# One place in the scheduler's order for all matmuls of a projection's PSUM tile, in a two-block transformer kernel

## The chip, the cores and the metric

The kernel runs on one core of one Trainium2 chip, in one launch. The metric is the device time of one execution in microseconds (us), taken as the median over several executions. The core has TensorE (PE) for matmuls, VectorE (DVE), ScalarE (ACT) and GpSimd (POOL) for elementwise work, SyncE (SP), which mostly issues DMAs, and 16 DMA engines. In the profile PEld is the loading of TensorE's stationary operand, which overlaps the matmuls.

## The reference

512 tokens of width 1024 go through two blocks, all in fp32. The first block has two layers; each has four attention kinds side by side and a feed-forward part of width 4096:

```python
for l in range(DEPTH):                       # 2 layers
    h = rms_norm(x, norm1[l])
    proj = h @ w_in[l]                       # 1024 x 2764, split into 16 parts
    ...                                      # o_a latent, o_b window, o_c top-k, o_d forget-gate attention
    x = x + mixed @ w_out[l]
    h2 = rms_norm(x, norm2[l])
    x = x + jnp.square(jax.nn.relu(h2 @ w_up[l])) @ w_down[l]
```

The second block normalizes x (with a scale and shift made from a condition vector by the ada weights), projects it to the parts of a gated delta rule (8 heads, chunks of 64), of a dilated window attention (12 heads) and to gates, and ends with three output projections whose results are combined and normalized.

## The kernel before, in words

**A projection.** Activations are kept transposed, channels on the 128 partitions and the 512 tokens in the free dimension. One output tile of a projection is 128 channels by 512 tokens in one PSUM bank, the tile `g`; `gtile` (line 139) gives it out of three buffers. To keep fp32 precision, every operand is split into a high and a low part of the reduced type fp32r. `split` (lines 122 to 136) does this for the weights: ACT copies the raw chunk to `whi` (line 130), and the remainder `wlo` is made by DVE (line 133) or POOL (line 135); each has three buffers (`split_bufs`), in the down projections of the feed-forward part four (`db`, tags `dh` and `dl`). The activations are split into `hh` and `hl` (line 160/161) or, in the feed-forward part, `sh` and `sl`. `gemm` (lines 141 to 152) then issues, for each 128-deep slice k of the inner dimension, three matmuls of 128x128 by 128x512: high by high (line 149), high weights by low activations (line 150), low weights by high activations (line 151). With 8 slices a tile has 24 matmuls, in `e_out` and the down projections with 4 slices it has 12. Weights come from HBM in pieces of 1 MB or less into `raw`, which has two buffers.

**The order of the work.** The program text only lists the operations. A list scheduler, which simulates the engines while the program is built, puts each engine's instructions into a fixed order; among instructions that it deems ready it takes the one with the smallest priority number. The number is a counter, `cur_priority`, that goes up by one with each instruction issued in the text. `gemm` raises it by `gp` (700 in the first block, 600 in the second) so that projections fill gaps left by the chains of the attention, and sets it back to its old value at the end (line 152). So the matmuls of one tile get rising numbers, `old + gp`, `old + gp + 1` and on, and the next projection, issued a handful of instructions later in the text, starts its numbers only a few places above the first one's start. On the chip each engine then takes its instructions in the fixed order.

**The stages.** The page's time runs through: attention of layer one (0 to 340 us), its feed-forward part (340 to 700), attention of layer two (700 to 1010), its feed-forward part, in which DVE also works off the ada products (1010 to 1385), the second block (1385 to 2000) and the final stage (from 2000). An attention stage begins with projections of the indexer's queries, of small pieces and of the latents (`qi`, `misc`, `Aq`, `Ak` in the list at line 815). `e_out` (line 802) adds the output projection to x and sums squares (`sumsq_add`, lines 166 to 172: ACT squares, POOL adds). The feed-forward part loops over 8 chunks of 512 hidden channels: `up(ch + 1)`, four tiles whose results DVE takes out of PSUM (line 860), and then `down(ch)`, eight tiles that DVE adds into `xT` (line 882). The last chunk has no `up` ahead of its `down`. After each layer, a matmul with ones (`ssp`, line 179, or line 996 at the end of the second layer) sums the squares over the channels. In two places the projections are not by `gemm`: `values` (line 549) and the delta block's V for the first group (line 1444), where `old` is read once and four tiles are issued in a loop.

Of the kernel before, what the change touches and what calls it, by code (L numbers as in the profile page):

```python
# [43 lines left out]
class Kernel:  # L44
# [96 lines left out]
    def gemm(self, ps, wk, acts, nk, first=True, last=True):  # L141

        nc = self.nc
        old = self.tc.cur_priority
        self.tc.cur_priority = old + self.gp
        for k in range(nk):
            wh, wl = wk(k)
            ah, al = acts(k)
            nc.tensor.matmul(ps, wh, ah, start=first and k == 0, stop=False)  # L149
            nc.tensor.matmul(ps, wh, al, start=False, stop=False)  # L150
            nc.tensor.matmul(ps, wl, ah, start=False, stop=last and k == nk - 1)  # L151
        self.tc.cur_priority = old


    def fold(self, x, g, d):
# [234 lines left out]
    def attn(self, l, hs, ssq, xin, xout):  # L390
# [30 lines left out]
        def raw_in(off, n=256):  # L421
            return self.raw(w_in[:, off:off + n], KD, n)
# [126 lines left out]
        def values(off):  # L549
            raw = raw_in(off)  # L550
            his = []
            for kk in range(2):
                his.append(self.split([(full, raw[:, 4 * kk:4 * kk + 4, :])], [P, 4, 256], lo=los.pop(0)))
            V = ap.tile([P, NB, 256], F32, name=self.nm("V"), tag="V", bufs=2)
            old = self.tc.cur_priority
            for b in range(NB):
                ps = self.gtile()
                self.tc.cur_priority = old + self.gp
                for k in range(KD):
                    wh, wl = (t[:, k % 4, :] for t in his[k // 4])  # L560
                    ah, al = (t[:, HB(b)] for t in hs[k])
                    nc.tensor.matmul(ps[:, :256], ah, wh, start=k == 0, stop=False)  # L562
                    nc.tensor.matmul(ps[:, :256], ah, wl, start=False, stop=False)
                    nc.tensor.matmul(ps[:, :256], al, wh, start=False, stop=k == KD - 1)
                self.tc.cur_priority = old
                nc.scalar.activation(V[:, b, :], ps[:, :256], AF.Copy, scale=S["rnat"][:, b:b + 1])
            return V
# [127 lines left out]
        def e_DV():  # L695
            S["VD"] = values(O_DV)
# [78 lines left out]
        def e_CV():  # L775
            S["VC"] = values(O_CV_)
# [655 lines left out]
    def g_Dv(self, gi, hs):  # L1432
        nc = self.nc
        w = self.I["w_in_2"][0]
        c0 = 4112 + 1536 + 256 * gi
        raw = self.raw(w[:, c0:c0 + 256], KD, 256)
        V = self.dst[gi]["V"] = self.da.tile([P, NB, 256], F32, name=self.nm("V"), tag="V", bufs=1)
        if gi:
            for j in range(2):
                t = self.residues(self.proj2(raw, slice(j * P, (j + 1) * P), hs), gi)  # L1440
                nc.scalar.activation(V[:, :, j * P:(j + 1) * P], self.natural(t), AF.Copy)
                yield
            return
        his = [self.split([(lambda t: t, raw[:, 4 * kk:4 * kk + 4, :])], [P, 4, 256], lo="v") for kk in range(2)]
        old = self.tc.cur_priority
        for b in range(NB):
            sel = lambda t: t[:, b * P:(b + 1) * P]
            ps = self.gtile()
            self.tc.cur_priority = old + self.gp
            for k in range(KD):  # L1450
                wh, wl = (t[:, k % 4, :] for t in his[k // 4])
                ah, al = (sel(t) for t in hs[k])
                nc.tensor.matmul(ps[:, :256], ah, wh, start=k == 0, stop=False)
                nc.tensor.matmul(ps[:, :256], ah, wl, start=False, stop=False)
                nc.tensor.matmul(ps[:, :256], al, wh, start=False, stop=k == KD - 1)
            self.tc.cur_priority = old
            nc.scalar.activation(V[:, b, :], ps[:, :256], AF.Copy)
            if b % 2:
                yield
# [341 lines left out]
```

## Time and profile before

| | |
|---|---|
| median of 3 runs | 2178.02 us (2175.59 to 2180.3) |
| the profiled execution | 2177.57 us, its span 2175.8 us |
| mean granted TensorE clock, share of full speed | 0.979 |
| PE busy | 2035.3 us, 94% of the span |
| DVE, ACT, POOL busy | 60%, 45%, 16% |
| DMA | 243.97 MB, mean 112 GB/s |
| chain that ended last | PE 65%, DVE 17%, DMA 6%, ACT 6%, issue 4%, POOL 2% |

The span is the time from the first to the last instruction of the profiled execution. TensorE's matmuls are pipelined, and a matmul's shown duration overlaps the next one's; what a matmul costs is read as the distance between two starts. A number in brackets behind a timeline entry is the time that the engine stood still ahead of it, with the instruction that released it.

### The profile page before, as it was taken

How to read it: one execution, taken by the hardware profiler on the slowest of the kernel's cores; microseconds unless marked ns; L12 is line 12 of the kernel's file. 1: busy time of each engine (PE TensorE's matmuls, PEld its weight loads, DVE VectorE, ACT ScalarE, POOL GpSimd, SP SyncE). 2: the span in 40 equal slices, each digit the busy share in tenths (PEclk: the TensorE clock that was granted, in tenths of full speed). 3: DMA queues.
4: the chain of work that ended last, by engine and by line, in shares of the span. 5: the costliest groups of instructions: out<-in, count | busy, mean ns of one | idle time of the engine just before them, and what ended most of it. 6: DMA issues, size and time to landing. Idle time of an engine off the chain costs nothing.

```text
span 2175.8 us, 27326 instructions
## 1 busy us (share of the span) xinstructions
PE 2035.3 (94%) x10015; PEld 1574.6 (72%) x10015; DVE 1315.3 (60%) x2372; ACT 973.6 (45%) x1769; POOL 350.5 (16%) x282
## 2 busy tenths in 40 slices
PE   6988989999999898999999999799999999999798
PEld 5776767777777676776777777577667767777576
DVE  6488764444444578855665554785484684763554
ACT  4546654222323454754332223563565655645332
POOL 5226320000003324511000000310102011000000
PEclk8999999999999999999999999999999999999899
DMA  5332443223323342352543433232213222244762
GB/s 173 99 102 73 132 145 116 78 79 98 115 78 93 98 110 78 93 167 81 172 149 125 136 116 108 69 98 80 75 64 97 76 71 89 87 139 159 263 207 97
DMA packets 230647, 243.97 MB, mean 112 GB/s; under 512 B 43771, under 2 KB 186026, under 8 KB 230514
## 3 DMA queue, kind: packets, MB, share of 16 engines
q1 hardware_dynamic: 227826, 240.13, 35.6%
q10 hardware_dynamic: 2688, 2.10, 0.3%
q8 instruction: 79, 1.29, 0.2%
q14 instruction: 54, 0.44, 0.1%
HBM read 203.93 MB, written 31.04 MB: 108 GB/s over the span
## 4 chain that ended last, share of the span: by engine, by line
PE 65%; DVE 17%; DMA 6%; ACT 6%; issue 4%; POOL 2%; SPq 0%; DVEq 0%; ACTq 0%; POOLq 0%
PE g L149 16%; PE g L150 15%; PE g L151 15%; DVE wlo L133 3%; PE oT L322 2%; DMA raw<-in_w_up_dram 1%; DVE X L1271 1%; PE pt L313 1%; DMA raw<-in_ada_w_dram 1%; DVE pr L1269 1%; ACT whi L130 1%; PE g L562 1%; PE S L678 1%; DVE m L543 1%; PE S L386 1%
## 5 line engine op out<-in xcount | busy, mean ns | idle before, releaser
L130 ACT ACTIVATE whi<-raw 128x1024 fp32r<-128x1024 f32 (+3 forms) x302 | 297.8, 1001 | 661.6 <-PE g L150 450.8
L149 PE MATMUL g<-hh,whi 128*128 128x512 f32 (+1 forms) x1368 | 497.7, 405 | 16.0 <-ACT whi L130 3.1
L151 PE MATMUL g<-hh,wlo 128*128 128x512 f32 x1368 | 487.5, 400 | 7.9 <-DVE wlo L133 7.8
L150 PE MATMUL g<-hl,whi 128*128 128x512 f32 x1368 | 490.4, 399 | 0.0
L133 DVE TENSOR_TENSOR wlo<-raw,whi 128x1024 fp32r<-128x1024 f32 (+4 forms) x258 | 309.2, 1212 | 129.6 <-ACT whi L130 114.0
L149 PEld LDWEIGHTS g<-hh,whi 128*128 128x128 f32 (+1 forms) x1368 | 259.3, 190 | 93.2 <-issue 15.6
L151 PEld LDWEIGHTS g<-hh,wlo 128*128 128x128 f32 x1368 | 258.1, 189 | 69.0 <-DVE wlo L133 10.0
L150 PEld LDWEIGHTS g<-hl,whi 128*128 128x128 f32 x1368 | 259.4, 190 | 55.2 <-issue 3.7
L149 PE MATMUL g<-sh,whi 128*128 128x512 f32 x512 | 195.5, 404 | 8.4 <-DVE xT L882 6.6
L150 PE MATMUL g<-sl,whi 128*128 128x512 f32 x512 | 190.9, 392 | 0.0
L151 PE MATMUL g<-sh,wlo 128*128 128x512 f32 x512 | 187.7, 391 | 0.0
L135 POOL TENSOR_TENSOR wlo<-raw,whi 128x1024 fp32r<-128x1024 f32 x44 | 107.1, 2435 | 424.7 <-ACT whi L130 284.2
L882 DVE TENSOR_TENSOR xT<-xT,g 128x512 f32<-128x512 f32 x128 | 85.8, 686 | 133.7 <-PE g L151 133.5
L149 PEld LDWEIGHTS g<-sh,whi 128*128 128x128 f32 x512 | 95.9, 188 | 48.6 <-DVE xT L882 22.6
L172 POOL TENSOR_TENSOR ssq<-sq,ssq 128x512 f32<-128x512 f32 x35 | 52.2, 1493 | 446.4 <-ACT sq L171 445.7
L860 DVE SCALAR_TENSOR_TENSOR r<-g,rstd 128x512 f32<-128x512 f32 x64 | 43.9, 690 | 122.3 <-PE g L151 122.3
L151 PEld LDWEIGHTS g<-sh,wlo 128*128 128x128 f32 x512 | 96.1, 188 | 21.4 <-DVE wlo L133 0.3
L150 PEld LDWEIGHTS g<-sl,whi 128*128 128x128 f32 x512 | 96.2, 188 | 17.9
L310 ACT ACTIVATE L<-L,mn 128x256 f32<-128x256 f32 (+3 forms) x128 | 68.4, 536 | 41.6 <-DVE mn L309 40.9
L318 ACT ACTIVATE ptsb<-pt 128x256 f32<-128x256 f32 (+3 forms) x128 | 50.9, 412 | 41.7 <-PE pt L313 38.5
L322 PE MATMUL oT<-ptsb,V 128*64 128x128 f32 x592 | 65.8, 289 | 3.2 <-ACT mx L575 3.1
L861 ACT ACTIVATE r<-r 128x512 f32<-128x512 f32 x64 | 40.0, 629 | 47.1 <-DVE r L860 46.9
(447 smaller groups left out, 3289.1 us busy)
## 6 DMA issues: line engine op xcount, KB each, us to landing
raw<-in_w_in_dram SPq DMA_DIRECT2D x46, 1024.0 KB
raw<-in_w_up_dram SPq DMA_DIRECT2D x32, 1024.0 KB
raw<-in_w_down_dram SPq DMA_DIRECT2D x32, 1024.0 KB
raw<-in_ada_w_dram SPq DMA_DIRECT2D x12, 1024.0 KB
raw<-in_w_in_dram SPq DMA_DIRECT2D x22, 512.0 KB
raw<-in_w_out_dram SPq DMA_DIRECT2D x32, 256.0 KB
fd<-f SPq DMA_DIRECT2D x30, 256.0 KB
xd<-xT SPq DMA_DIRECT2D x24, 256.0 KB
```

Source lines behind the costliest of these rows:

```text
L130: nc.scalar.activation(f(hi), src, AF.Copy)
L133: nc.vector.tensor_tensor(f(lw), src, f(hi), ALU.subtract)
L135: nc.gpsimd.tensor_tensor(f(lw), src, f(hi), ALU.subtract)
L149: nc.tensor.matmul(ps, wh, ah, start=first and k == 0, stop=False)
L150: nc.tensor.matmul(ps, wh, al, start=False, stop=False)
L151: nc.tensor.matmul(ps, wl, ah, start=False, stop=last and k == nk - 1)
L172: nc.gpsimd.tensor_tensor(ssq, sq, ssq, ALU.add)
L310: nc.scalar.activation(L[:, :n], L[:, :n], AF.Exp, bias=m, scale=-1.0, accum_out=sm[:, hh, i:i + 1])
L318: nc.scalar.activation(pts_[:, :n], pt[:, :n], AF.Copy)
L322: nc.tensor.matmul(oT[hh * 64:(hh + 1) * 64, i * P:(i + 1) * P], V(hh, j0 + jj), pts[hh][:, jj * P:(jj + 1) * P], start=jj == 0, stop=jj = ...
L860: nc.vector.scalar_tensor_tensor(r, ps, 0.0, rstd, ALU.max, ALU.mult)
L882: nc.vector.tensor_tensor(x, x, ps, ALU.add)
```

## The change

A method `later(old)` sets the counter to `old + gp`, and it is called ahead of every matmul of a projection instead of once ahead of the tile's first one. All 24 (or 12) matmuls of a tile thus carry the same number; the next tile's number is higher, since its `old` is. No instruction, shape or buffer changes, only the order.

```diff
--- before.py
+++ after.py
@@ -142,14 +142,20 @@
 
         nc = self.nc
         old = self.tc.cur_priority
-        self.tc.cur_priority = old + self.gp
         for k in range(nk):
             wh, wl = wk(k)
             ah, al = acts(k)
+            self.later(old)
             nc.tensor.matmul(ps, wh, ah, start=first and k == 0, stop=False)
+            self.later(old)
             nc.tensor.matmul(ps, wh, al, start=False, stop=False)
+            self.later(old)
             nc.tensor.matmul(ps, wl, ah, start=False, stop=last and k == nk - 1)
         self.tc.cur_priority = old
+
+    def later(self, old):
+
+        self.tc.cur_priority = old + self.gp
 
 
     def fold(self, x, g, d):
@@ -555,12 +561,14 @@
             old = self.tc.cur_priority
             for b in range(NB):
                 ps = self.gtile()
-                self.tc.cur_priority = old + self.gp
                 for k in range(KD):
                     wh, wl = (t[:, k % 4, :] for t in his[k // 4])
                     ah, al = (t[:, HB(b)] for t in hs[k])
+                    self.later(old)
                     nc.tensor.matmul(ps[:, :256], ah, wh, start=k == 0, stop=False)
+                    self.later(old)
                     nc.tensor.matmul(ps[:, :256], ah, wl, start=False, stop=False)
+                    self.later(old)
                     nc.tensor.matmul(ps[:, :256], al, wh, start=False, stop=k == KD - 1)
                 self.tc.cur_priority = old
                 nc.scalar.activation(V[:, b, :], ps[:, :256], AF.Copy, scale=S["rnat"][:, b:b + 1])
@@ -1446,12 +1454,14 @@
         for b in range(NB):
             sel = lambda t: t[:, b * P:(b + 1) * P]
             ps = self.gtile()
-            self.tc.cur_priority = old + self.gp
             for k in range(KD):
                 wh, wl = (t[:, k % 4, :] for t in his[k // 4])
                 ah, al = (sel(t) for t in hs[k])
+                self.later(old)
                 nc.tensor.matmul(ps[:, :256], ah, wh, start=k == 0, stop=False)
+                self.later(old)
                 nc.tensor.matmul(ps[:, :256], ah, wl, start=False, stop=False)
+                self.later(old)
                 nc.tensor.matmul(ps[:, :256], al, wh, start=False, stop=k == KD - 1)
             self.tc.cur_priority = old
             nc.scalar.activation(V[:, b, :], ps[:, :256], AF.Copy)
```

The places below show TensorE's instructions in the order of before and of the changed kernel. A name's number tells apart the tiles; in the changed kernel lines 150 and 151 of before are lines 151 and 153. The numbers in g, sh, sl, whi and wlo are the same tiles in both.

The first place is the end of the second layer's last down projection: g_10878, g_10892 and g_10906 are the last three of its eight tiles, and ssp_10950 the sum over channels of the squares of the finished x. TensorE before:

```order
L150 MATMUL g_10906<-sl_10587,whi_10800 128x512
L150 MATMUL g_10878<-sl_10623,whi_10804 128x512
L149 MATMUL g_10892<-sh_10622,whi_10804 128x512
L151 MATMUL g_10906<-sh_10586,wlo_10801 128x512
L151 MATMUL g_10878<-sh_10622,wlo_10805 128x512
L150 MATMUL g_10892<-sl_10623,whi_10804 128x512
L149 MATMUL g_10906<-sh_10622,whi_10804 128x512
L151 MATMUL g_10892<-sh_10622,wlo_10805 128x512
L150 MATMUL g_10906<-sl_10623,whi_10804 128x512
L151 MATMUL g_10906<-sh_10622,wlo_10805 128x512
L996 MATMUL ssp_10950<-ssqb,ones 128x512
```

TensorE after the change:

```order
L149 MATMUL g_10906<-sh_10548,whi_10794 128x512
L151 MATMUL g_10906<-sl_10549,whi_10794 128x512
L153 MATMUL g_10906<-sh_10548,wlo_10795 128x512
L149 MATMUL g_10906<-sh_10586,whi_10800 128x512
L151 MATMUL g_10906<-sl_10587,whi_10800 128x512
L153 MATMUL g_10906<-sh_10586,wlo_10801 128x512
L149 MATMUL g_10906<-sh_10622,whi_10804 128x512
L151 MATMUL g_10906<-sl_10623,whi_10804 128x512
L153 MATMUL g_10906<-sh_10622,wlo_10805 128x512
L1004 MATMUL ssp_10950<-ssqb,ones 128x512
```

Before, the three tiles take turns and all end within the last six matmuls ahead of ssp; now the last tile's matmuls stand together, and g_10892 and g_10878 ended 12 and 24 matmuls ahead of its end.

The second place is the start of layer one's attention: g_274 and g_303 are the two halves of the indexer's queries, g_342 the small pieces. TensorE before:

```order
L151 MATMUL g_274<-hh_156,wlo_271 128x512
L149 MATMUL g_303<-hh_156,whi_299 128x512
L149 MATMUL g_274<-hh_169,whi_270 128x512
L150 MATMUL g_303<-hl_157,whi_299 128x512
L149 MATMUL g_342<-hh_119,whi_334 128x512
L150 MATMUL g_274<-hl_170,whi_270 128x512
L151 MATMUL g_303<-hh_156,wlo_300 128x512
L150 MATMUL g_342<-hl_120,whi_334 128x512
L151 MATMUL g_274<-hh_169,wlo_271 128x512
L149 MATMUL g_303<-hh_169,whi_299 128x512
```

TensorE after the change:

```order
L151 MATMUL g_274<-hl_196,whi_270 128x512
L153 MATMUL g_274<-hh_195,wlo_271 128x512
L149 MATMUL g_274<-hh_208,whi_270 128x512
L151 MATMUL g_274<-hl_209,whi_270 128x512
L153 MATMUL g_274<-hh_208,wlo_271 128x512
L149 MATMUL g_303<-hh_119,whi_299 128x512
L151 MATMUL g_303<-hl_120,whi_299 128x512
L153 MATMUL g_303<-hh_119,wlo_300 128x512
```

Three tiles were open at once; now g_274 is finished ahead of the first matmul of g_303. Before, g_274 has its last matmul 33 places further on.

The third place is the boundary between the last two down projections of layer one, where no up projection stands between: g_5300 and g_5314 belong to `down(6)`, g_5348 and g_5362 to `down(7)`; whi_5212 is the last of the four weight tiles of `down(6)`, whi_5330, whi_5334 and whi_5340 are the first three of `down(7)`. TensorE before:

```order
L149 MATMUL g_5314<-sh_4912,whi_5212 128x512
L150 MATMUL g_5348<-sl_5083,whi_5330 128x512
L151 MATMUL g_5300<-sh_4912,wlo_5213 128x512
L150 MATMUL g_5314<-sl_4913,whi_5212 128x512
L151 MATMUL g_5348<-sh_5082,wlo_5331 128x512
L151 MATMUL g_5314<-sh_4912,wlo_5213 128x512
L149 MATMUL g_5348<-sh_5118,whi_5334 128x512
L150 MATMUL g_5348<-sl_5119,whi_5334 128x512
L151 MATMUL g_5348<-sh_5118,wlo_5335 128x512
L149 MATMUL g_5348<-sh_5156,whi_5340 128x512
L150 MATMUL g_5348<-sl_5157,whi_5340 128x512
L149 MATMUL g_5362<-sh_5082,whi_5330 128x512
```

TensorE after the change:

```order
L151 MATMUL g_5314<-sl_4913,whi_5212 128x512
L153 MATMUL g_5314<-sh_4912,wlo_5213 128x512
L149 MATMUL g_5348<-sh_5082,whi_5330 128x512
L151 MATMUL g_5348<-sl_5083,whi_5330 128x512
L153 MATMUL g_5348<-sh_5082,wlo_5331 128x512
L149 MATMUL g_5348<-sh_5118,whi_5334 128x512
L151 MATMUL g_5348<-sl_5119,whi_5334 128x512
L149 MATMUL g_5362<-sh_5082,whi_5330 128x512
L153 MATMUL g_5348<-sh_5118,wlo_5335 128x512
L149 MATMUL g_5348<-sh_5156,whi_5340 128x512
L151 MATMUL g_5348<-sl_5157,whi_5340 128x512
L151 MATMUL g_5362<-sl_5083,whi_5330 128x512
```

Before, g_5348 was begun among the last matmuls of `down(6)`; now it starts behind the whole of g_5314, and the list scheduler lets g_5362 in among it.

## Rows read from the trace of the kernel before

**Rows 1.** The profile's page: part 1 (busy time), part 5 (groups of instructions)

```profile
PE 2035.3 (94%) x10015; PEld 1574.6 (72%) x10015; DVE 1315.3 (60%) x2372; ACT 973.6 (45%) x1769; POOL 350.5 (16%) x282
...
L135 POOL TENSOR_TENSOR wlo<-raw,whi 128x1024 fp32r<-128x1024 f32 x44 | 107.1, 2435 | 424.7 <-ACT whi L130 284.2
```

**Rows 2.** Windows by stage: window, us, busy us of each engine, PEclk, DMA

```profile
0.00:340.00 340.00, 300.59 (x1609) 233.29 (x1610) 230.03 (x468) 177.89 (x380) 128.88 (x108) 0.96 0.39 116
340.00:700.00 360.00, 355.64 (x1509) 276.90 (x1508) 167.28 (x198) 116.05 (x147) 17.36 (x12) 1.00 0.31 99
...
1385.00:2000.00 615.00, 584.04 (x3119) 446.31 (x3118) 395.90 (x801) 345.89 (x642) 78.47 (x70) 0.98 0.30 89
2000.00:2176.00 176.00, 150.87 (x694) 117.21 (x692) 91.93 (x135) 53.86 (x92) 2.37 (x1) 0.94 0.56 190
```

**Rows 3.** Waits of TensorE: waiting <- awaited: us in total, times, longest

```profile
PE g L149 <- DVE sg L1664: 13.6, 1, 13.6
...
PE ssp L179 <- POOL ssq L172: 7.7, 3, 2.8
...
PE g L149 <- DVE xT L882: 6.6, 5, 1.8
...
PE ssp L996 <- DVE ssqb L994: 5.0, 1, 5.0
...
PE g L149 <- DVE qn L426: 3.9, 2, 1.9
...
PE g L149 <- DVE xT L802: 2.7, 5, 0.8
...
PE is L526 <- POOL qi L520: 2.5, 4, 1.0
...
PE g L149 <- DVE ra L277: 2.4, 2, 1.3
```

**Rows 4.** Timeline at 40 us: start, us, instruction, [idle <- releaser]

```profile
39.53 2.12 DVE L133 TENSOR_TENSOR wlo<-raw,whi 128x1024 fp32r<-128x1024 f32 x1
...
40.67 0.39 PE L150 MATMUL g<-hl,whi 128*128 128x512 f32 x1
40.90 0.39 PE L151 MATMUL g<-hh,wlo 128*128 128x512 f32 x1
...
41.57 0.68 DVE L277 TENSOR_TENSOR ra<-g,cosr 128x512 f32<-128x512 f32 x1
...
42.40 0.47 PE L149 MATMUL g<-hh,whi 128*128 128x512 f32 x1 [1.11 <-DVE ra L277]
```

**Rows 5.** Timeline, end of the second layer, at 1369 us

```profile
1368.70 1.96 DVE L882 TENSOR_TENSOR xT<-xT,g 128x512 f32<-128x512 f32 x3 [2.24 <-PE g L151]
...
1369.18 0.39 PE L150 MATMUL g<-sl,whi 128*128 128x512 f32 x1
1369.41 0.39 PE L151 MATMUL g<-sh,wlo 128*128 128x512 f32 x1
...
1370.59 4.03 DVE L994 TENSOR_TENSOR ssqb<-bsq,ssqb 128x512 f32<-128x512 f32 x3
...
1374.76 2.05 PE L996 MATMUL ssp<-ssqb,ones 128*128 128x512 f32 x2 [4.96 <-DVE ssqb L994]
```

**Rows 6.** Timeline, start of the first feed-forward part, at 321 us

```profile
322.09 1.23 ACT L171 ACTIVATE sq<-xT 128x512 f32<-128x512 f32 x2 [0.90 <-DVE xT L802]
...
322.86 3.66 POOL L172 TENSOR_TENSOR ssq<-sq,ssq 128x512 f32<-128x512 f32 x2 [2.02 <-ACT sq L171]
...
326.58 2.08 PE L179 MATMUL ssp<-ssq,ones 128*128 128x512 f32 x2 [2.83 <-POOL ssq L172]
```

**Rows 7.** Timeline, feed-forward part of the second layer, at 1285 us

```profile
1285.57 0.50 PE L149 MATMUL g<-sh,whi 128*128 128x512 f32 x1 [1.74 <-DVE xT L882]
```

**Rows 8.** Timeline, ACT and DVE in the last down projection of layer one

```profile
666.08 3.90 ACT L130 ACTIVATE whi<-raw 128x1024 fp32r<-128x1024 f32 x4 [12.64 <-PE g L150]
...
670.65 2.35 DVE L133 TENSOR_TENSOR wlo<-raw,whi 128x1024 fp32r<-128x1024 f32 x2
```


## The prediction

> **What bounds the kernel now.** I read the busy times first: TensorE is busy 94% of the span, no other engine more than 60% [rows 1]. So what the change can give has to come out of TensorE's standing time, and that differs by stage [rows 2]: in the attention stage of layer one TensorE's busy time leaves 39.4 of 340 us open, in the feed-forward part of that layer only 4.4 of 360, in the second block 31 of 615, in the final stage 25 of 176. A feed-forward stage therefore has almost nothing to give inside, only at its ends. Then I read what TensorE waits for [rows 3]. The longest wait, 13.6 us in the final stage, is for a value that comes back through DMA; no projection order decides it, and I leave it as it is. The rows that the change can touch directly are those where the awaited operation takes a projection's result out of PSUM, or is the end of a chain that begins there: 7.7 (squares summed at the layer's end), 6.6 (down tiles added to x), 5.0 (the same squares at the second block's start), 3.9 and 2.5 (chains of the latents and the indexer's queries), 2.7 (the output projection added to x) and 2.4 (the query rotation), together 30.8 us.
>
> **What a change of tile costs by itself: nothing.** Inside one tile the starts stand 0.23 us apart, from 40.67 to 40.90, where the order has only g_342 [rows 4]; between matmuls of different tiles it is 0.23 us too, from 1369.18 to 1369.41, g_10906 behind g_10892 and its neighbours [rows 5]. Since no instruction is added or removed, the number of matmuls times 0.23 us stays, and the sum is one of waits alone.
>
> **Layer ends.** At 1369 us the three last down tiles end together. DVE needs 1.96 us for three additions and then 4.03 us for the three additions of squares, and TensorE stands 4.96 us ahead of ssp [rows 5]. With the change only the last tile is unfinished when TensorE stops: one addition 1.96/3 = 0.65, one ACT square about 1.23/2 = 0.61 (taken from the like operation of rows 6), one addition 4.03/3 = 1.34, and some 0.3 us for handing over: 2.9 us in place of 5.0. Gain 2.1. At 321 us and twice more the adder is POOL, 3.66/2 = 1.83 us an addition [rows 6]; two late tiles give the chain 3.66 behind ACT's first square, and TensorE stands 2.83. With one late tile it is 0.65 + 0.61 + 1.83 + 0.3 = 3.4 us after the tile's end, of which the 10 to 12 matmuls of the next projection that the new order puts ahead of ssp cover 2.3 to 2.8. So 0.6 to 1.1 stays of each; of the 7.7 us of the three places some 2.6. Gain 5.1. The bounds of both terms together are 0 and the 12.7 us of their rows.
>
> **Banks.** Where a projection's first matmul waits for DVE's addition, as at 1285.57 for 1.74 us [rows 7], the three banks are finished nearly together, so the fourth tile's bank comes free late. In the new order a bank is asked for again two whole tiles after its own end, 2 x 12 x 0.23 = 5.5 us for a down tile, 11 for an up tile, which is over twice the longest of these waits (1.8). I take 5.5 of the 6.6 us. At 42.40 TensorE waits 1.11 us for the first rotation product, which stands behind a 2.12 us remainder on DVE [rows 4]; there g_303's end is 24 matmuls = 5.5 us ahead of the tile that wants a bank, and the 2.4 us of both layers go. Of the output projection's 2.7 us, five short waits behind the same kind of addition, I take 1.2. Of the 3.9 and 2.5 us of the latents' chains half, 3.2: their projections end earlier one after another, but the waiting matmul moves forward in the order as well. The sum of gains is 2.1 + 5.1 + 5.5 + 2.4 + 1.2 + 3.2 = 19.5 us, bounds 0 and 30.8.
>
> The Trainium skill ("Perfetto Trace Analysis", section Matmuls) asks for independent matmul groups that rotate through different PSUM banks, so that the evacuation of one overlaps the matmuls of the next. Before, three groups rotate matmul by matmul and are evacuated in a bunch [rows 5]; tiles that end one after another let it work again. Taken as a rule without a rest, all 21.7 us of the rows for both ssp, for xT of the down tiles and for ra would go, where my terms have 15.1.
>
> **New costs.** First the boundary of the last two down projections. Four weight tiles must be replaced there; ACT needs 3.90 us for the four high parts, DVE 2.35 us for two remainders, 4.7 for four [rows 8]. Before, the matmuls of g_5314 and g_5300 took turns and g_5348 was spread over them. Now buffer k comes free only in the last tile's own slice k, the first one nine matmuls or 2.1 us ahead of its end. From that release it takes one ACT copy, 3.90/4 = 0.98, and four remainders, 4.7, until the fourth is ready: 5.7 us, so 3.6 us after the tile's end, and 4.9 if DVE's additions of two finished tiles to x (0.65 each) come between. The scheduler mixes g_5362 into g_5348 over the slices that are there, so TensorE asks for the fourth remainder some 17 matmuls, 3.9 us, behind that end: a wait of 1.0, with some handing over at the earlier slices 1.5 us. That at two boundaries (one in each layer) is 3.0; bounds 0 and 2 x 4.7 = 9.4. Second, the order puts the first scores of the top-k attention (made from Cq and Ck) 20 places later, while the heads before it come earlier; bound by 0 and by 20 x 0.23 = 4.6 us in each layer; I take 1.0 each, as other projections fill most of it. Third, the second block: its events move by up to some ten matmuls either way; I take 1.5 lost, bounds 5 gained and 8 lost, by the size of its longest wait in rows 3. The sum of losses is 3.0 + 2.0 + 1.5 = 6.5 us.
>
> **The sum.** 2177.6 of the profiled execution, less 19.5, plus 6.5 gives 2164.6; its time is 0.45 us below the median of the runs shown, so 2165 us.
>
> **Rivals.** (a) Nothing that can be measured: a change under 0.2% (4.4 us) is what a measurement of this kernel can't tell from none. TensorE takes its instructions in order, so a wait taken away can come back whole at the next instruction that awaits a DVE, POOL or DMA chain; the attention stages, where most standing time is, are full of such chains (39.4 us open, and DVE busy 230 of 340) [rows 2]. For it speaks that the 13.6 us wait of the final stage shows a chain which no order of tiles shortens; against it that at 1369 and 321 us nothing is queued that could take the time up. It gives 2174 to 2182.
> (b) Slower: one tile at a time leaves TensorE nothing else to turn to when that tile's weights are late. A tile's third matmul needs the remainder, now 2 x 0.23 = 0.46 us after the tile's start; with three tiles taking turns it came up to 1.4 us after it. POOL needs 2.435 us for a remainder, 44 times [rows 1]. If each second one of these is late by the 0.9 us of difference, 22 x 0.9 = 20 us are lost against my 13, which makes 2185; it decides from some 14 of the 44 late ones. For it: the bound on what the spread forgave is real at 44 places. Against it: POOL stood idle 424.7 us ahead of them, mostly for ACT, and three weight buffers run up to two tiles of 5.5 us ahead.
> The Trainium skill ("TensorE: Matmul & The Clock Gate", section Step-by-step: what each phase is for) says that matmuls stay in program order and only weight loads are pulled ahead. That speaks against the change in just this way; the traces bear out the standing still (4.96 us with other weights at hand), not yet its price.
> (c) More than forecast: if all of the 30.8 us goes, the time is 2177.6 - 30.8 + 6.5 = 2153; and fewer stops could give back some of the granted clock, 0.96 in the first 340 us and 0.94 in the last 176 (a mix of the two levels, 2.4 and 1.2 GHz), where each hundredth missing is worth 3.4 and 1.8 us [rows 2]: a third of 13.6 + 10.6 is 8 us more, 2145.
> (d) The change doesn't do what it says: the loops of values and of the delta block's first V read `old` once, so four tiles carry one number and stay mixed. That touches few tiles, and the time would hardly show it; it has no chance of its own.
>
> **How the numbers follow.** The forecast 0.50, its own range 2156 to 2173; nothing measurable (a) 0.17; slower (b) 0.19; more (c) 0.14, 2141 to 2156. The range 2146 to 2184 leaves out half of (b)'s upper part and a little of (c). Faster: 0.48 + 0.14 + 0.03 = 0.65. Same: 0.02 + 0.13 + 0.02 = 0.17. Slower: 0.01 of (a) and 0.17 of (b), 0.18.
>
> **What would show it.** In the profile after: the wait ahead of ssp at the second block's start near 3 us and at the three others near 1; no wait of a projection for the additions to xT above 1 us, none at 42 us for the rotation; a new wait of 1 to 2 us for a weight remainder at the start of the last down projection, twice. Wrong would be the forecast if the waits for remainders grow by more than 10 us in all (then b), or if these rows shrink and the stage's length stays (then a), which would show at the start of the feed-forward part: it should begin some 5 us earlier than before.

## The result and the profile after

The changed kernel takes 2146.09 us (median of 4 runs, 2142.94 to 2148.97), the kernel before 2179.16 in the same comparison; the ratio is 0.9843, 95% interval 0.9824 to 0.9861. That is 30 to 38 us less; 13 were forecast. The direction was right, the size was not, and the time lies at the range's lower end (2146).

From the page after (part 1, and from part 5 the weight loads at the head of a down tile's slice: busy, mean ns | idle before, releaser; "issue" is time in which an engine waited for nothing that the profile shows):

```profile
PE 2011.2 (94%) x10015; PEld 1588.6 (74%) x10015; DVE 1303.4 (61%) x2372; ACT 970.4 (45%) x1769; POOL 347.0 (16%) x282
...
L149 PEld LDWEIGHTS g<-sh,whi 128*128 128x128 f32 x512 | 96.5, 189 | 20.9 <-issue 0.9
```

TensorE's share is 94% as before [rows 1], although 34.6 us are gone from the span: its busy time itself fell by 24.1 us. The same matmuls can't do less work. A matmul is shown 0.39 us long while they start 0.227 apart, so a start that is up to 0.16 us late leaves no idle time in the row. These are the rows of before that I should have read side by side, matmul and weight load of the same line:

```profile
L149 PE MATMUL g<-sh,whi 128*128 128x512 f32 x512 | 195.5, 404 | 8.4 <-DVE xT L882 6.6
...
L149 PEld LDWEIGHTS g<-sh,whi 128*128 128x128 f32 x512 | 95.9, 188 | 48.6 <-DVE xT L882 22.6
```

The matmuls of that line show 8.4 us of idle time, their weight loads 48.6, of which 22.6 were waits for the addition to xT; after, the weight loads show 20.9 and no such wait.

The windows by stage, cut at the sums over channels (ssp): four stretches before (attention and feed-forward part of each layer, from the first ssp at 23.3 us), then the same four after, from 21.3 us, and the rest. Columns as in [rows 2].

```profile
23.30:326.60 303.30, 276.59 (x1527) 214.48 (x1525) 212.85 (x450) 161.99 (x355) 115.10 (x86) 0.98 0.37 110
326.60:698.40 371.80, 367.44 (x1544) 285.93 (x1544) 167.75 (x199) 117.60 (x148) 17.36 (x12) 0.99 0.30 96
698.40:998.20 299.80, 273.07 (x1515) 212.03 (x1515) 210.65 (x451) 162.16 (x357) 110.40 (x83) 0.98 0.36 107
998.20:1374.80 376.60, 365.32 (x1567) 286.93 (x1567) 212.78 (x310) 112.83 (x146) 12.04 (x8) 0.99 0.40 129
```

```profile
21.30:321.10 299.80, 276.36 (x1524) 215.48 (x1524) 205.54 (x450) 162.00 (x356) 113.53 (x86) 0.97 0.37 111
321.10:675.70 354.60, 352.73 (x1541) 290.26 (x1541) 170.25 (x199) 113.73 (x148) 16.65 (x12) 0.99 0.32 101
675.70:975.70 300.00, 276.75 (x1517) 215.86 (x1517) 206.74 (x451) 162.38 (x357) 108.12 (x83) 0.96 0.36 107
975.70:1344.90 369.20, 361.03 (x1568) 292.43 (x1569) 212.49 (x310) 112.97 (x146) 11.22 (x8) 0.99 0.41 132
1344.90:2141.20 796.30, 734.99 (x3827) 567.57 (x3827) 492.80 (x946) 405.44 (x741) 82.71 (x72) 0.97 0.36 111
```

Up to the first ssp, while the inputs load, 2.0 us are gone (23.3 to 21.3); they are not the change's, since this ssp starts at 21.3 us in a later kernel with the order of before there (mixed_5banks) and at 23.0 in one with the order of after (evac2_seq). Layer one's attention lost 3.5 us (303.3 to 299.8), the first feed-forward part 17.2 (371.8 to 354.6), layer two's attention nothing (299.8, 300.0), the second feed-forward part 7.4, the rest 4.7. Most of the gain is in the stages that I had called nearly full.

TensorE's waits after, with the lines that answer to [rows 3]:

```profile
PE g L149 <- DVE sg L1674: 15.7, 1, 15.7
PE ssp L185 <- POOL ssq L178: 11.6, 4, 4.7
PE S L392 <- ACT kh L367: 5.5, 2, 2.8
PE g L149 <- DVE qn L432: 5.5, 2, 2.8
...
PE A L1243 <- DVE qd L1167: 4.4, 4, 2.9
...
PE ssp L1004 <- DVE ssqb L1002: 3.5, 1, 3.5
...
PE S L393 <- POOL qk L383: 2.0, 2, 1.3
...
PE g L149 <- DVE xT L810: 1.4, 2, 0.7
...
PE is L532 <- POOL qi L526: 0.5, 2, 0.2
```

The waits for xT of the down tiles (6.6) and for ra (2.4) are gone, L1004 is 3.5 (5.0 before), xT of the output projection 1.4 (2.7), is 0.5 (2.5). But ssp behind POOL went from 7.7 to 11.6, qn from 3.9 to 5.5, and others that were small or absent stand there now (S behind kh 5.5, A behind qd 4.4). Other waits of the score matmuls (S) shrank: those for qk fell from 6.7 to 2.0.

What the first feed-forward part's weight loads wait for (us in total, times, longest), before and then after; after, the rows left are the layer's end and one remainder:

```profile
PEld g L149 <- DVE xT L882: 10.8, 30, 1.7
PEld g L149 <- DVE r L860: 4.7, 14, 0.8
PEld g L149 <- ACT whi L130: 3.6, 10, 0.4
PEld g L149 <- issue: 3.4, 12, 0.3
```

```profile
PEld g L153 <- DVE wlo L133: 0.3, 1, 0.3
```

One such late start before. Columns: start, us, engine, instruction, idle before.

```profile
423.56 0.40 PE L151 MATMUL g<-sh,wlo 128*128 128x512 f32 x1
...
424.00 0.69 DVE L882 TENSOR_TENSOR xT<-xT,g 128x512 f32<-128x512 f32 x1 [2.69 <-PE g L151]
424.03 0.39 PE L150 MATMUL g<-sl,whi 128*128 128x512 f32 x1
...
424.26 0.40 PE L151 MATMUL g<-sh,wlo 128*128 128x512 f32 x1
...
424.74 0.19 PEld L149 LDWEIGHTS g<-sh,whi 128*128 128x128 f32 x1 [0.51 <-DVE xT L882]
424.74 0.50 PE L149 MATMUL g<-sh,whi 128*128 128x512 f32 x1
424.84 0.19 PEld L150 LDWEIGHTS g<-sl,whi 128*128 128x128 f32 x1
425.07 0.40 PE L150 MATMUL g<-sl,whi 128*128 128x512 f32 x1
...
425.31 0.40 PE L151 MATMUL g<-sh,wlo 128*128 128x512 f32 x1
```

A down tile's last matmul starts at 423.56; DVE, idle until then, adds the tile from 424.00 to 424.69; the next tile takes its bank, and its first weight load is at 424.74, together with its matmul instead of some 0.2 us ahead. The matmuls start at 424.26, 424.74, 425.07, 425.31: 0.48 and 0.33 instead of 0.23 twice, 0.35 us lost, and no matmul row has a bracket. In the order after, a weight load looks like this, here inside an up tile:

```profile
405.14 0.39 PE L149 MATMUL g<-hh,whi 128*128 128x512 f32 x1
405.15 0.19 PEld L151 LDWEIGHTS g<-hl,whi 128*128 128x128 f32 x1
405.37 0.39 PE L151 MATMUL g<-hl,whi 128*128 128x512 f32 x1
```

The load at 405.15 is 0.22 us ahead of its matmul at 405.37. Summed over the first feed-forward part without its ends, the distances between matmul starts that exceed 0.227 us exceed it by 15.6 us before and by 0.6 after. Before, these were 73 distances of 60 to 150 ns over it (7.7 us), 343 of 5 to 60 (3.8) and ten longer ones (4.0). The waits of the weight loads, 22.5 us in the four rows above, are more than this loss, since a load normally has some 0.2 us in hand.

### The profile page after: what moved, and what is told of

Read it like the earlier page. It is cut to its first block, busy times and chain, and to the rows that moved or that the text cites. A ratio compares the mean times of both kernels' runs of the same rounds, so it can differ in the third digit from the quotient of the medians.

```text
span 2141.2 us, 27281 instructions
## 1 busy us (share of the span) xinstructions
PE 2011.2 (94%) x10015; PEld 1588.6 (74%) x10015; DVE 1303.4 (61%) x2372; ACT 970.4 (45%) x1769; POOL 347.0 (16%) x282
## 4 chain that ended last, share of the span: by engine, by line
PE 41%; DVE 11%; DMA 5%; ACT 4%; issue 2%; POOL 1%; SPq 0%; DVEq 0%; ACTq 0%; POOLq 0%
PE g L149 10%; PE g L153 10%; PE g L151 10%; DVE wlo L133 2%; ACT whi L130 1%; DMA raw<-in_w_out_dram 1%; PE oT L328 1%; DVE X L1279 1%; DMA raw<-in_ada_w_dram 1%; DVE ada L967 1%; PE oT L1513 1%; DVE pr L1277 1%; PE nt L1174 1%; PE pt L319 1%; PE g L1709 1%
## 5 line engine op out<-in xcount | busy, mean ns | idle before, releaser
L149 PE MATMUL g<-hh,whi 128*128 128x512 f32 (+1 forms) x1368 | 548.3, 401 | 5.9 <-ACT whi L130 3.0
L153 PE MATMUL g<-hh,wlo 128*128 128x512 f32 x1368 | 546.3, 399 | 3.9 <-DVE wlo L133 3.9
L151 PE MATMUL g<-hl,whi 128*128 128x512 f32 x1368 | 548.1, 401 | 0.0
L133 DVE TENSOR_TENSOR wlo<-raw,whi 128x1024 fp32r<-128x1024 f32 (+4 forms) x258 | 300.3, 1178 | 108.9 <-ACT whi L130 100.1
L149 PE MATMUL g<-sh,whi 128*128 128x512 f32 x512 | 200.6, 392 | 0.0
L151 PE MATMUL g<-sl,whi 128*128 128x512 f32 x512 | 200.2, 392 | 0.0
L153 PE MATMUL g<-sh,wlo 128*128 128x512 f32 x512 | 199.8, 392 | 0.0
L149 PEld LDWEIGHTS g<-sh,whi 128*128 128x128 f32 x512 | 96.5, 189 | 20.9 <-issue 0.9
L149 PE MATMUL g<-yh,whi 128*128 128x512 f32 x112 | 44.7, 404 | 15.7 <-DVE sg L1674 15.7
```

The costliest lines, as they stand in the source:

```text
L133: nc.vector.tensor_tensor(f(lw), src, f(hi), ALU.subtract)
```

## Experiments

Theory A: the surplus is won in the feed-forward parts, where mixed tiles end together and the next tile's weight load waits for its bank. Theory B: it is won in the chains of the attention and the second block. "Part 1" and "part 2" are the two feed-forward parts, from ssp to ssp in the profile; ratios are to the kernel before.

| kernel | median us | ratio, 95% interval | part 1 | part 2 |
|---|---|---|---|---|
| before | 2175 to 2179 | | 371.8 | 376.6 |
| changed | 2146.09 | 0.9843 (0.9824 to 0.9861) | 354.6 | 369.2 |
| ffn_only | 2147.77 | 0.9879 (0.9859 to 0.9900) | 353.4 | 366.0 |
| rest_only | 2175.97 | 0.9996 (0.9980 to 1.0012) | 371.3 | 377.7 |
| down_only | 2162.12 | 0.9934 (0.9917 to 0.9951) | 360.7 | 366.7 |
| mixed_5banks | 2169.40 | 0.9969 (0.9953 to 0.9984) | 365.6 | 373.7 |
| mixed_2banks | 2200.54 | 1.0099 (1.0069 to 1.0129) | 381.7 | 388.9 |
| seq_2banks | 2151.63 | 0.9863 (0.9835 to 0.9890) | 354.7 | 368.3 |
| evac2_mixed | 2175.18 | 0.9986 (0.9971 to 1.0001) | 371.2 | 376.5 |
| evac2_seq | 2156.00 | 0.9893 (0.9862 to 0.9925) | 356.0 | 369.9 |
| pairs_5banks | 2143.82 | 0.9857 (0.9836 to 0.9878) | 354.9 | 366.3 |
| pairs_2banks | 2195.48 | 1.0097 (1.0079 to 1.0114) | 383.6 | 394.7 |
| fold_late5 | 2140.64 | 0.9839 (0.9823 to 0.9856) | 354.1 | 366.0 |

**Where the gain is.** A switch in `later`, set around the up and down projections only, around everything else, or around the down projections only:

```diff
     def later(self, old):
-        self.tc.cur_priority = old + self.gp
+        if self.seq:
+            self.tc.cur_priority = old + self.gp
...
+            self.seq = True        # False in rest_only, True in down() alone in down_only
             sq = up(0)
```

> One place per tile only in the up and down projections of both feed-forward parts; all other projections as before. Theory A (the surplus over the forecast is won inside the feed-forward parts, where weight loads at the head of a tile waited for its PSUM bank): first feed-forward part about 355 us long as in the changed kernel (before 371.8), second about 369 (before 376.6), in all 20 to 26 us below before, some 2155. Theory B (the gain comes from the attention's and the second block's chains, the feed-forward parts only inherit it): within 6 us of before, 2172 to 2180.

> The opposite half: one place per tile everywhere except in the up and down projections. Theory A: the feed-forward parts stay at about 372 and 377 us, the whole is 6 to 12 us below before (2167 to 2173). Theory B: 28 us or more below before, about 2148.

> One place per tile only in the down projections. If the wait for the additions to xT (the down tiles' own evacuation, 10.8 us of weight-load waits in the first feed-forward part) is what was paid, this alone gives most of it: first feed-forward part 358 to 362 us, in all 14 to 20 us below before. If mixed up tiles or their weight buffers were the price (waits for r 4.7, whi 3.6), it gives under 6 us.

Theory B fell: the feed-forward parts alone bring 26 us (1.21%), both parts as long as in the changed kernel or shorter. The down tiles alone bring 11.1 us of part 1 and 9.9 of part 2, nearly all of the 10.6 of ffn_only; the up tiles the remaining 7 of part 1. The rest alone changes nothing that can be measured, where theory A had expected 6 to 12 us of it. The halves' 26 and 1 us don't quite add up to the 34 of both; the profiled spans do more nearly (30.0 and 2.4 us below before, 34.6 for both), and the intervals are some 4 us wide each.

The rest did change, as the windows show: first layer one's attention in rest_only (order of the changed kernel), then in mixed_2banks (a kernel below, with the order of before in this stage).

```profile
21.60:325.80 304.20, 281.34 (x1523) 218.71 (x1523) 206.74 (x450) 162.05 (x355) 113.51 (x86) 0.95 0.36 110
```

```profile
21.40:328.00 306.60, 279.76 (x1525) 217.14 (x1525) 211.02 (x450) 161.77 (x355) 115.51 (x86) 0.97 0.37 109
```

TensorE stood still 22.9 us in rest_only and 23.4 in the changed kernel, against 26.7 before. But the granted clock of this stretch, a mix of the two levels (1.2 and 2.4 GHz), was 0.95 and 0.97 against 0.98, and the matmuls took longer: busy 281.3 us in rest_only against 276.6 before. At the same granted clock, 0.97, the changed kernel's stage is 6.8 us shorter than that of mixed_2banks (299.8, 306.6). Over whole executions the granted clock was 0.966 to 0.976 in all runs of the kernels with one place per tile outside the feed-forward parts, and 0.974 to 0.982 in all of the others. So one place per tile does take standing time out of the attention, and a lower clock goes with it and takes much of that back. Why the clock was lower no run shows.

**Banks or turns.** The up and down tiles take their PSUM tile from other tags (a tag names a group of buffers: g has three banks, s two), in the mixed order of before (mixed) or of the changed kernel (seq; with two banks all but six of TensorE's instructions keep their place):

```diff
-                    ps = self.gtile()      # in up() and down()
+                    ps = self.ftile()
...
+    def ftile(self):
+        self.nf = getattr(self, "nf", -1) + 1
+        tag = "gsgsg"[self.nf % 5]         # "ss" and % 2 for two banks
+        return self.ps.tile([P, T], F32, name=self.nm("g"), tag=tag, bufs=3 if tag == "g" else 2)
```

> The mixed order of before, but the up and down tiles go round five PSUM banks (three of tag g, two of tag s) instead of three. If a scarce bank alone is the price of mixing, five banks pay it: the waits of the weight loads for the additions to xT and for r fall below 5 us together, the first feed-forward part is about 356 us, the whole some 18 us below before. If it is the bunching itself (tiles that take turns end together, however many), up to five tiles end together and the part stays above 366 us.

> The changed kernel's order, but up and down tiles go round two PSUM banks (tag s) instead of three. Theory A (one tile at a time needs a bank again only a whole tile of 2.7 us after its end, when the 0.69 us addition to xT is long done): first feed-forward part within 3 us of the changed kernel's 354.6. Rival (the changed kernel wins by the third bank's slack): waits for xT and r come back, the part grows to 362 or more.

> The order of before, but up and down tiles go round two PSUM banks, so at most two tiles take turns. Theory A (tiles that end together and ask for banks at once): more waits for xT than before (10.8 us in the first part), that part 375 us or more. Rival (depth of mixing, thus weights and orders, is the price): with two tiles in turn instead of three the part is shorter than 371.8, about 365.

With two banks the sequential order loses nothing in part 1 (354.7), the mixed one 9.9 us more than before. Weight loads between 345 and 690 us in mixed_2banks, then in mixed_5banks:

```profile
PEld g L154 <- DVE xT L887: 16.5, 22, 0.8
PEld g L154 <- DVE r L865: 9.0, 14, 1.0
```

```profile
PEld g L154 <- DVE xT L887: 3.9, 13, 0.4
PEld g L154 <- DVE r L865: 3.5, 12, 0.3
PEld g L156 <- DVE wlo L133: 2.4, 10, 0.2
```

Two banks raise the wait for xT from 10.8 to 16.5 us and for r from 4.7 to 9.0; five lower them to 3.9 and 3.5, but up to five tiles are then open and remainders of weights (2.4) are late too. 365.6 is nearer to bunching than to scarce banks alone, by the bound that I had set (366); it decides little by itself, since five banks also changed how many tiles are mixed. Part 1 falls in order with banks: 381.7, 371.8, 365.6.

**A longer addition.** Each down tile is added to x twice, first into a scratch tile:

```diff
+                    t2 = fp.tile([P, T], F32, name=self.nm("t2"), tag="r", bufs=3)
+                    nc.vector.tensor_tensor(t2, x, ps, ALU.add)
                     nc.vector.tensor_tensor(x, x, ps, ALU.add)
```

> The kernel before with each down tile's addition to xT done twice, first into a scratch tile, so that a bank is held 0.69 us longer and DVE has 128 x 0.69 = 88 us more work (64 of them in each part). Theory A: mixed tiles have no slack for it; each of some 45 late tile starts per part is up to 0.7 us later, the first part is 10 to 40 us longer than 371.8. Rival (DVE has room, 45% busy there): under 5 us.

> The same doubled addition in the changed kernel. Theory A: a bank is asked for again two tiles, 5.5 us, after its end; the first feed-forward part stays within 4 us of 354.6, the layer ends cost about 1 us more each. Rival (any order pays for a longer evacuation): 10 us or more longer.

The sequential kernel's part 1 grew by 1.4 us, as expected; its whole is some 10 us longer, of which only 2.1 are in the two parts and the rest isn't explained. The mixed one's part 1 didn't grow at all (371.2), against theory A as I had put it and with the rival's number. Its weight loads in part 1:

```profile
PEld g L149 <- issue: 7.7, 6, 1.3
PEld g L149 <- DVE r L860: 6.3, 21, 0.4
PEld g L149 <- ACT whi L130: 4.6, 10, 1.3
PEld g L149 <- DVE xT L884: 0.3, 1, 0.3
```

The waits for xT are nearly gone; others stand there, 18.9 us in these rows against 22.5 before. The list scheduler knows that the addition is longer and orders the next tile's start later (the scratch tile also shares r's three buffers, which blurs the rest). TensorE's fixed order shows this. From the first down tile of part 1 on, 88 tiles take over a bank from an earlier one. Counted in matmuls from the last one of the earlier tile to the first one of the next, the distance before is 4 to 11 places, and 5 in 54 of them. In the changed kernel it is 25 or more in 86, in seq_2banks 13 or more in 86. With the doubled addition in the mixed order it is 7 to 19 behind a down tile. The late start shown above is one of 4 places: at 0.227 us each that is 0.91 us, and the weight load came 1.18 us after the last matmul's start (423.56 to 424.74). So I take it that not the length of the evacuation is paid, but that the mixed order starts a tile as soon as its bank comes free by the scheduler's account, without a margin for what the chip needs more. I call that A'.

**Turns with and without margin.** To part taking turns from the missing margin, the down tiles run in pairs, the two of a pair in turns, pairs one after another, up tiles in sequence:

```diff
+            for j, (w, a) in enumerate(((wh, ah), (wh, al), (wl, ah))):
+                self.tc.cur_priority = base + self.gp + 3 * k + j   # base + 12 for the next pair
+                self.nc.tensor.matmul(ps, w, a, ...)
```

> The changed kernel, but the eight down tiles of a chunk run as four pairs, the two tiles of a pair in turns matmul by matmul, over five PSUM banks; up tiles one after another. Theory A' (what costs is a tile that starts just as its bank comes free, not the turns themselves): five banks give each bank a pair's time of rest, so the first feed-forward part is within 3 us of the changed kernel's 354.6. Rival (taking turns costs in itself): 256 down tiles' worth of turns, of which the first part has half, cost at least 6 us, part 361 or more.

> The same pairs over two PSUM banks: both tiles of a pair end together and the next pair asks for both banks at once. Theory A': 32 pair starts in the part, each 0.7 to 1.2 us late (one addition 0.69 and the hand-over), the part 22 to 40 us longer than with five banks, about 380 to 394. Rival (the scheduler hides it, or turns alone matter): the same as with five banks within 3 us.

With five banks 354.9, with two 383.6 (part 1 has 64 down tiles, not the 128 that the first expectation counts). Taking turns costs nothing there (the rival fell). With two banks 61 of the 88 tiles start 2 to 5 places behind the end of their bank's earlier tile, with five banks all stand 26 or more behind it; asking for the bank so soon costs 28.7 us in part 1. Weight loads of part 1 with two banks:

```profile
PEld g L154 <- DVE xT L907: 21.8, 23, 1.0
```

With five banks no weight load of a tile waits between 342 and 670 us. This shows what a missing margin costs, and that turns are free where there is one. That the 17.2 us of the change are this cost throughout is less sure: of the 22.5 us of waits before, 15.5 were for a bank (xT and r), and the other 7.0 for weights or for nothing that the profile shows. They too are gone after the change, and no run separates them from the banks.

**The layer's start, made worse by the change.** DVE, POOL and TensorE at 315 us in the changed kernel:

```profile
313.71 0.39 PE L153 MATMUL g<-mh,wlo 128*128 128x512 f32 x1
...
314.80 0.68 DVE L810 TENSOR_TENSOR xT<-xT,g 128x512 f32<-128x512 f32 x1
...
316.85 1.31 DVE L167 SCALAR_TENSOR_TENSOR hl<-xT,veccol,hh 128x512 fp32r<-128x512 f32 x1 [1.37 <-ACT hh L166]
318.09 0.67 DVE L810 TENSOR_TENSOR xT<-xT,g 128x512 f32<-128x512 f32 x1
...
319.63 1.39 POOL L178 TENSOR_TENSOR ssq<-sq,ssq 128x512 f32<-128x512 f32 x1 [2.02 <-ACT sq L177]
...
321.07 0.50 PEld L185 LDWEIGHTS ssp<-ssq,ones 128*128 128x128 f32 x2 [5.09 <-POOL ssq L178]
```

The last matmul of the output projection starts at 313.71, but the last tile's addition is at 318.09: DVE stood 1.37 us for ACT's hh and then made hl ahead of it. The addition, square and sum of the last tile end at 321.02, with TensorE standing 4.67 us. So fold_late5 lets the splits of x's tiles 5 and 6 go only behind the last addition:

```diff
+                self.last_add = nc.vector.tensor_tensor(x, x, ps, ALU.add)
...
+                    if 5 <= d < KD - 1:
+                        c2.enter_context(self.tc.issue_after(self.last_add.ins))
                     h2.append(self.fold(...))
```

> The changed kernel, but at the start of a feed-forward part the splits of x's tiles 5 and 6 (hh and hl) may only be issued behind the last addition of the output projection, so that DVE's additions aren't queued behind hl, which waits for ACT. If the 4.7 us wait for ssq there is DVE's order (add, split, add), the two waits of some 4.8 us shrink to 1 to 2.5 each and the whole is 4 to 7 us below the changed kernel (about 2140). If it is the chain of ACT and POOL, they stay above 4 and the time is the same.

In fold_late5:

```profile
314.53 0.69 DVE L810 TENSOR_TENSOR xT<-xT,g 128x512 f32<-128x512 f32 x1 [0.28 <-PE g L153]
...
317.20 1.54 POOL L178 TENSOR_TENSOR ssq<-sq,ssq 128x512 f32<-128x512 f32 x1 [0.79 <-ACT sq L177]
...
318.80 1.13 PE L185 MATMUL ssp<-ssq,ones 128*128 128x512 f32 x2 [2.25 <-POOL ssq L178]
```

The last addition is at 314.53 now, and the wait 2.25 us instead of 4.67; the like wait in layer two is 2.20 instead of 4.7. So it was DVE's order. A gain of the whole isn't shown: its median is 5.5 us below the changed kernel's (2140.64), but each was compared with other runs of the kernel before, and the ratios are level (0.9839 and 0.9843).

## Why the prediction was wrong in size

1. **The step that failed: "A feed-forward stage therefore has almost nothing to give inside, only at its ends."** It rested on 4.4 us of open time in 360, and with it went "the number of matmuls times 0.23 us stays, and the sum is one of waits alone". Busy time hides starts that are up to 0.16 us late: in part 1 some 11.5 us (7.7 and 3.8) were lost in steps of at most 0.15 us. Measured: 17.2 us in part 1 and 7.4 in part 2, where my terms give about 1 and 5 (the 5.5 us of the banks shared out by where their waits stand, 1.3 us of them in part 1, the ssp at the part's end, less 1.5 for the boundary).
2. **The term of the banks was mis-sized.** I took 5.5 us from the matmuls' row for xT (6.6). The mechanism was right, the row was the wrong one: the weight loads' row for the same wait has 22.6 us, and the up tiles' r and the weights come on top. The two whole tiles of rest that I counted on are there (25 places or more), and that such a margin is what counts is shown by pairs_5banks against pairs_2banks and by seq_2banks against mixed_2banks.
3. **Layer ends.** 5.1 us gain forecast for ssp behind POOL; it lost 3.9 (7.7 to 11.6). At the end of part 1 (698 us before) the wait fell only from 2.07 to 1.87, where I had expected 0.6 to 1.1 to stay; there too DVE makes an hl, for which it waits 0.79 us for ACT, ahead of the last tile's addition. At the two starts of a feed-forward part DVE's order set the end, as fold_late5 showed. My chain of one addition, one square and one sum left out the splits that the order puts in between. The second block's ssp came out at 3.5 for 2.9.
4. **Rotation and output projection.** 2.4 and 1.2 forecast, 2.4 and 1.3 measured. The latents' 3.2 came out as 0.4 (6.4 to 6.0).
5. **New costs.** The boundary of the last two down projections was to cost 3.0; the only wait of a weight load there is 0.3 us in each layer. The attention's later scores are seen in new waits (S behind kh, 5.5); all waits of score matmuls (S) together went from 14.4 to 16.1 us, which is 1.7 more.
6. **Rival (a)** has the number of rest_only, which was no faster than before, but not by its own mechanism alone. New waits did come there (ssp 11.1, qn 5.5, S behind kh 5.5), yet TensorE's standing time in the two attention stages fell from 53.4 to 46.0 us; what came back came with the lower granted clock. **(b)** did not come: the remainders' waits fell (7.8 to 3.9 us in the matmuls' rows). **(c)** has the time in its range, 2141 to 2156, by luck: the clock gave nothing back but fell, from 0.979 before to 0.975 after, and the waits of [rows 3] didn't all go.
7. What the Trainium skill says of rotating banks ("Perfetto Trace Analysis", Matmuls), that the evacuation of one group should overlap the next group's matmuls, agrees with the traces. The kernel before rotates through three banks too, but leaves 4 to 11 places for the evacuation. With 26 or more, in pairs_5banks, turns are free (354.9 us).

## What to carry to other kernels

Where an engine's instructions overlap in the trace, its busy share can't show small losses: compare the distance between starts with its undisturbed value, and read the waits of the weight loads, not only of the matmuls. Let tiles finish one by one when they share a few PSUM banks; a bank must be asked for again later than the addition and the hand-over take (here 0.78 us from the last matmul's end to the next weight load). A static scheduler that packs work just in time leaves no margin for what its model doesn't know. And before a stage is called unchanged, compare its granted clock as well as its length.

## What the runs showed of the hardware

A weight load that waited for its bank starts together with its matmul instead of some 0.2 us ahead, and not only this matmul is late but the next one too (0.48 and 0.33 us for 0.23). In part 1 of pairs_2banks this is so behind all 29 loads ahead of which the loading stood over 0.3 us: the start behind the late one follows after 0.31 to 0.34 us. Changing the PSUM bank with every matmul of the down tiles cost nothing that part 1 shows (354.9 us in turns, 354.6 in sequence).
